# Accumulating weight transfers begun before and after the latent attention instead of inside it, and a planner that counts transfers as longer

## The chip, the cores and the metric

One core of a Trainium2 chip runs the whole program in one launch. The metric is device time in microseconds; the value compared is the median of the runs of a kernel. TensorE multiplies, VectorE, ScalarE and GpSimd work element by element, SyncE only issues transfers. The rows of the profile call them PE, DVE, ACT, POOL and SP.

## The reference

Two transformer blocks in float32 over 1024 tokens of width 1024. Block 1: a Fourier mixing and a latent attention (MLA, 8 heads) side by side, a cross attention over 256 memory tokens, and 16 experts that each choose 128 tokens. Block 2: one wide projection, a convolution of 31 taps per channel, dilated attention in three groups, gates. Cut to what the change touches:

```python
h = _rmsnorm(x, norm_g[layer]) * (1.0 + scale) + shift
proj = h @ w_in[layer]                       # block 2: 1024 x 10240
(glu_a, glu_b, z_conv, q, k, v, z_att, g_conv, g_att) = jnp.split(proj, split_idx, axis=-1)
```

## The kernel before

The kernel is written as a recording: each call on an engine becomes an operation with a price (line 236: time on its engine, and a latency until another engine can use the result). A list scheduler (line 284 on) then plays the program through with these prices and fixes, for each engine, one order of operations; on the chip each engine works its queue off in that order, and a wait at its head holds all that stands behind. So a changed price or a moved call changes orders far away too. A transfer that SyncE begins is priced with 2.0 us of latency, an accumulating one that GpSimd begins (`add_dma`) with 3.5 us. All operations recorded that way carry the line number 180 in the profile; the adding transfers carry 1433.

The order of stages is: block 1's input projection (`block1_in`) and Fourier part, MLA, output mixing (`mix_out`) and memory attention, routing and experts, and then block 2. There the projection is computed for sixteen pairs of tiles (`in2_pair`) by seven products of quarter matrices each, in place of eight, 112 products in all. Each product loads a quarter weight `wq`, ScalarE casts its high half into `wqs`, VectorE subtracts to get the low half (also `wqs`), and TensorE does twelve matmuls (four blocks of 128, three each: high by high, high by low, low by high) into one PSUM bank `wp`. VectorE then adds or subtracts `wp` to outputs named by their part (`glu_a`, `z_conv`, `z_att`, `g_att`). Between these operations VectorE also does the convolution's taps (`conv`), whose due time is set late by a constant, so they fill its gaps.

Four of the seven quarter weights of a pair are sums of quarters of the weight matrix. They are made in DRAM during block 1, since nothing needs them before block 2: for each pair a sum t13 = w2a + w2b and a sum t24 = w2a + w2d + w2c, half of which also gets a part of w_in. `weight_sums` is a generator that yields one step at a time: a copy of w2a (on SyncE's queue, 32 of them) or an accumulating transfer (on GpSimd's queue, 64 of them: 16 each of w2b, w2d, w2c and w_in). A sum's adds depend on each other, each begins when the one before has landed, and they wait at the head of GpSimd's queue. `sum_step(m)` takes the next m steps and stands at chosen places of the program. Before, the places are block 1's input projection (steps of 2 and 3), the Fourier loops (1) and each quarter of each MLA head (2, thirty-two times), and a last call takes what is left.

In MLA, GpSimd also scales the probabilities: for each head and each 128 queries TensorE computes scores `s`, the softmax gives `p` with its `sum`, GpSimd multiplies `p` by the reciprocal of the sum, TensorE transposes (`pt`) and multiplies by the values (`o`), which goes to `ya`. GpSimd also makes low halves of weights there (`wl`, `ql`, `kl`).

Of the kernel before, what the change touches and what calls it, by code (L numbers as in the profile page):

```python
# [188 lines left out]
class Program:  # L189
# [55 lines left out]
    def price(self, eng, fn, a, kw, wr, rd):  # L245

        out = wr[0] if wr else None
        if fn == "dma_start":
            v = next(x for x in list(a) + list(kw.values()) if isinstance(x, V))
            b = 4 * int(np.prod(v.shape))  # L250
            return max(0.45, b / 360e3), 2.0
        n = max([x.free for x in wr + rd if x is not None] or [1])
        if eng == "pe":
            m = rd[0]
# [339 lines left out]
class Kern(Program):  # L594
# [242 lines left out]
    def block1_in(self):  # L837
# [28 lines left out]
        for name, m0, n in (("q_lat", 4, 3), ("kv_lat", 7, 2)):  # L866
            tiles, acc = [], None
            for i in range(n):
# [9 lines left out]
                tiles.append((h, l))  # L878
                self.sum_step(2)
                if acc is not None:  # L880
# [41 lines left out]

        self.sum_step(2)
        self.uf = []
        for m in range(4):
            w = self.wtile(a["w_in"][m], 8)
            u = self.page("uf")
            self.gemm_t(w, xs, lambda t, ps: self.dve.tensor_tensor(u[:, t], ps, rxb[:, t], OP.mult), base="uf")
            self.out_dbg("uf", u, m)
            self.sum_step(3)  # L930
            self.uf.append(u)
# [107 lines left out]
    def mla(self):  # L1039
# [23 lines left out]
        for h in range(8):  # L1063
# [21 lines left out]
            for qq in range(4):  # L1085
                if 4 * h + qq in MEM_AT:
                    next(mem, None)
                self.sum_step(2)
                pth = [self.page("pth", F32R, (P, 4, 256)) for _ in range(2)]
# [25 lines left out]
        for _ in mem:  # L1115
            pass
        self.sum_step(1000)

# [14 lines left out]
    def mix_out(self, yf, x1d):  # L1133
# [5 lines left out]
        for m in range(8):  # L1139
# [4 lines left out]
            self.x1.append(x)  # L1144
            self.out_dbg("x1", x, m)

    def mem_stats(self):
# [46 lines left out]
    def mem_attention(self, x1d):  # L1194
# [8 lines left out]
        for m in range(8):  # L1203
# [4 lines left out]
            self.gemm_t(w, xs, lambda t, ps: self.act.copy(q[:, t], ps), base="mq")  # L1208
            qf.append(q)
            for _ in range(3):  # L1210
                n = len(self.ops)
                next(ada, None)
                for op in self.ops[n:]:
                    op.deps.add(n - 1)
# [11 lines left out]
        for hd in range(4):  # L1226
# [6 lines left out]
            for g in range(2):  # L1233
# [21 lines left out]
                for dm in range(2):  # L1255
# [6 lines left out]
                    self.split_to(oh[dm][0][:, t], oh[dm][1][:, t], o, lo="dve")  # L1262
            os[hd] = oh
            for part in PARTS:
                if part[-1] == hd:
# [164 lines left out]
    def add_dma(self, out, x):  # L1430

        def issue():
            self.nc.gpsimd.dma_start(out=out.ap(), in_=x.ap() if isinstance(x, V) else x, accum_op=OP.add,
                                     **({"max_dma_last_dim": 2048} if out.t.kind == "dram" else {}))
        op = self.record("pool", 1.0, 3.5, issue, [out] + [x] * isinstance(x, V), [out])
        op.dma = 4 * int(np.prod(out.shape)) / 180e3
        return op

    def sum_step(self, m):
        n = len(self.ops)  # L1440
        self.bias = 200
        for _ in range(m):
            next(self.sums, None)
        self.bias = 0
# [3 lines left out]
    def weight_sums(self):  # L1448


        a, n = self.a, len(PAIRS)
        self.t13 = [self.dram_tile((P, NT), "t13") for _ in PAIRS]
        self.t24 = [self.dram_tile((P, NT), "t24") for _ in PAIRS]
        R = slice(512, NT)
        for i in range(n + 3):
            if i < n:
                self.sp.dma_start(self.t13[i], a["w2a"][i], max_dma_last_dim=2048)
                yield
                self.sp.dma_start(self.t24[i], a["w2a"][i], max_dma_last_dim=2048)
                yield  # L1460
            if 0 <= i - 1 < n:
                self.add_dma(self.t13[i - 1], a["w2b"][i - 1])
                yield
                self.add_dma(self.t24[i - 1], a["w2d"][i - 1])
                yield
            if 0 <= i - 2 < n:
                self.add_dma(self.t24[i - 2], a["w2c"][i - 2])
                yield
            if 0 <= i - 3 < n:
                p, m = PAIRS[i - 3][0]  # L1470
                self.add_dma(self.t24[i - 3][:, R], a["w_in2"][IN2[p] + m][:, 4:].rearrange("p k c -> p (k c)"))
                yield

# [740 lines left out]
```

## Time and profile before

| | us |
|---|---|
| three runs | 2776.07, 2768.86, 2770.32 |
| median | 2770.32 |
| the profiled execution, its own time | 2776.95 |
| its span, first to last instruction | 2775.1 |
| TensorE busy in it | 2632.8 (95%) |
| VectorE, ScalarE, GpSimd busy | 2124.6, 1396.0, 497.8 |
| mean granted TensorE clock | 0.972 |

The rows further down come from this one execution. The windows view gives each engine's busy time and its count of instructions between two times of the span, with the granted clock. The waits view groups an engine's idle time by what it waited for. A timeline lists instructions with their start, length and, in brackets, the idle time before them and what ended it.

### The profile page before, as it was taken

The numbers are of one execution on the slowest core, as the hardware profiler recorded it, in microseconds if no ns is written. First come the engines' busy times: TensorE is split into PE (matmuls) and PEld (weight loads), VectorE is DVE, ScalarE is ACT, GpSimd is POOL, SyncE is SP. The second block draws the span as 40 slices with busy tenths as digits, with TensorE's granted clock in tenths as the row PEclk, the third lists the DMA queues.
The fourth block names the chain that finished last, engine by engine and source line by source line (L and its number), as shares of the span: only waits on it lengthen the run. The fifth ranks groups of instructions, "written<-read, shape, count | busy, mean of one in ns | idle before, by whom it ended". The sixth has DMA issues, their size and how long they took to land. (4 is left out here: it accounts for less than half of the span.)

```text
span 2775.1 us, 36565 instructions
## 1 busy us (share of the span) xinstructions
PE 2632.8 (95%) x13038; PEld 2202.8 (79%) x13038; DVE 2124.6 (77%) x3225; ACT 1396.0 (50%) x2280; POOL 497.8 (18%) x347
## 2 busy tenths in 40 slices
PE   8999989999994999999997999989999999998998
PEld 6888878888884888888876888768888887786877
DVE  7367876547666899988886998669999998669563
ACT  6156666432344777777776433334545455434211
POOL 2136558311004040000000000001111112001000
PEclk9999999999997999999998999999999999998999
DMA  7556565534537899999993333455556658678841
GB/s 243 145 123 121 131 157 140 193 109 155 200 107 278 316 345 366 351 374 374 391 346 118 114 114 120 139 158 127 135 133 137 148 128 244 161 215 300 320 171 53
DMA packets 178936, 555.18 MB, mean 200 GB/s; under 512 B 20179, under 2 KB 22419, under 8 KB 178753
## 3 DMA queue, kind: packets, MB, share of 16 engines
q1 hardware_dynamic: 150144, 481.53, 49.0%
q0 software_dynamic: 28608, 71.31, 14.0%
q8 instruction: 103, 1.69, 0.2%
q14 instruction: 81, 0.66, 0.1%
HBM read 439.02 MB, written 118.98 MB: 201 GB/s over the span
## 5 line engine op out<-in xcount | busy, mean ns | idle before, releaser
L180 DVE SCALAR_TENSOR_TENSOR conv<-glu_b,convw,conv 128x1023 f32<-128x1023 f32 (+14 forms) x210 | 268.0, 1277 | 2.6
L180 DVE TENSOR_TENSOR w_upl<-w_up,w_uph 128x1024 fp32r<-128x1024 f32 x128 | 149.2, 1220 | 23.0 <-ACT w_uph L180 22.4
L180 DVE TENSOR_TENSOR w_downl<-w_down,w_downh 128x1024 fp32r<-128x1024 f32 x128 | 149.0, 1219 | 13.5 <-ACT w_downh L180 12.9
L180 ACT CAST wqs<-wq 128x512 fp32r<-128x512 f32 x112 | 68.8, 621 | 167.6 <-PE wp L180 64.0
L180 DVE TENSOR_TENSOR w_gatel<-w_gate,w_gateh 128x1024 fp32r<-128x1024 f32 x123 | 144.0, 1218 | 7.5 <-ACT w_gateh L180 4.8
L180 PE MATMUL wp<-h2h,wqs 128*128 128x512 f32 x384 | 123.8, 396 | 9.6 <-ACT wqs L180 9.6
L180 ACT CAST w_gateh<-w_gate 128x1024 fp32r<-128x1024 f32 x128 | 125.6, 1053 | 6.4 <-issue 2.9
L180 ACT CAST w_downh<-w_down 128x1024 fp32r<-128x1024 f32 x128 | 126.0, 1055 | 1.4 <-PE ea L180 1.4
L180 ACT CAST w_uph<-w_up 128x1024 fp32r<-128x1024 f32 x128 | 125.8, 1055 | 1.4 <-PE ea L180 0.7
L180 ACT ACTIVATE ap<-ap,amx 128x128 f32<-128x128 f32 (+1 forms) x192 | 85.5, 449 | 68.9 <-DVE amx L180 62.0
L180 POOL MEMSET kl<- 64x1024 f32 x24 | 22.8, 951 | 475.5 <-PE wp L180 258.5
L180 POOL TENSOR_TENSOR wl<-w,wh 128x1024 fp32r<-128x1024 f32 (+3 forms) x31 | 61.7, 1990 | 244.5 <-ACT wh L180 227.5
L180 ACT CAST wh<-w 128x1024 fp32r<-128x1024 f32 (+3 forms) x71 | 62.4, 896 | 77.1 <-DMA w<-in_w_convout_dram 35.2
L180 DVE TENSOR_TENSOR ptl<-pt,pth 128x512 fp32r<-128x512 f32 x128 | 81.8, 683 | 19.5 <-ACT pth L180 12.9
L180 PEld LDWEIGHTS wp<-h2h,wqs 128*128 128x128 f32 x384 | 73.4, 191 | 25.9 <-ACT wqs L180 10.4
L180 ACT CAST w2h<-w 128x1024 fp32r<-128x1024 f32 x48 | 50.1, 1048 | 76.3 <-DMA w<-in_w_in_dram 60.3
L180 DVE TENSOR_TENSOR wqs<-wq,wqs 128x512 fp32r<-128x512 f32 x112 | 75.5, 685 | 16.5 <-ACT wqs L180 16.4
L180 ACT ACTIVATE p<-p,mx 128x1024 f32<-128x1024 f32 x64 | 73.8, 1155 | 26.1 <-DVE mx L180 17.5
L180 POOL TENSOR_SCALAR p<-p,sum 128x1024 f32<-128x1024 f32 x64 | 75.2, 1234 | 55.2 <-DVE sum L180 51.9
L180 PE MATMUL ea<-w_gatel,hth 128*128 128x512 f32 x256 | 80.1, 394 | 0.4 <-DVE w_gatel L180 0.4
L180 PE MATMUL ea<-w_gateh,hth 128*128 128x512 f32 x256 | 80.5, 395 | 0.0
L180 PE MATMUL eb<-w_uph,hth 128*128 128x512 f32 x256 | 80.5, 394 | 0.1
(626 smaller groups left out, 8623.0 us busy)
## 6 DMA issues: line engine op xcount, KB each, us to landing
w_gate<-in_w_gate_dram SPq DMA_DIRECT2D x128, 512.0 KB
w_up<-in_w_up_dram SPq DMA_DIRECT2D x128, 512.0 KB
w_down<-in_w_down_dram SPq DMA_DIRECT2D x128, 512.0 KB
w<-in_w_in_dram SPq DMA_DIRECT2D x57, 512.0 KB
w2l<-w POOLq DMA_DIRECT2D x36, 512.0 KB, 6.7
t<-in_w2a_dram SPq DMA_DIRECT2D x32, 512.0 KB
wq<-t SPq DMA_DIRECT2D x64, 256.0 KB
wada<-in_w_adaT_dram SPq DMA_DIRECT2D x24, 512.0 KB
```

The source lines that it names most:

```text
L180: getattr(k.engines[eng], fn)(*[r(x) for x in a], **{n: r(x) for n, x in kw.items()})
```

## The change

Five things are edited. The latency that the planner counts for a transfer goes from 2.0 to 2.8 us, that of an adding transfer from 3.5 to 5.5. The generator is split into one for copies and one for adds, and `sum_step` says from which it takes. Inside MLA only copies are taken, one for each quarter of a head. Adds are taken in block 1's later projection loop and the Fourier loops, and then after MLA: two for each of the eight tiles of `mix_out`, one for each of eight steps of the memory query projection, five after each of four memory heads. The last call, which took everything left, is gone. By the orders of the two kernels, 21 adds stand ahead of MLA before and 43 in it; of the changed kernel's 64, 20 stand ahead of it, none in it, and 44 behind it. Of the 32 copies, 14 then stand ahead of MLA and 18 in it.

```diff
         if fn == "dma_start":
...
-            return max(0.45, b / 360e3), 2.0
+            return max(0.45, b / 360e3), 2.8
...
                 self.gemm_t(w, xs, evac, base="u")
                 tiles.append((h, l))
-                self.sum_step(2)
+                self.sum_step(2, True)
...
-        self.sum_step(2)
+        self.sum_step(4, True)
         self.uf = []
         for m in range(4):
...
-            self.sum_step(3)
+            self.sum_step(2)
...
             for qq in range(4):
                 if 4 * h + qq in MEM_AT:
                     next(mem, None)
-                self.sum_step(2)
+                self.sum_step(1, True)
...
         for _ in mem:
             pass
-        self.sum_step(1000)
...
             self.out_dbg("x1", x, m)
+            self.sum_step(2)
...
             qf.append(q)
+            self.sum_step(1)
...
             os[hd] = oh
+            self.sum_step(5)
...
-        op = self.record("pool", 1.0, 3.5, issue, [out] + [x] * isinstance(x, V), [out])
+        op = self.record("pool", 1.0, 5.5, issue, [out] + [x] * isinstance(x, V), [out])
...
-    def sum_step(self, m):
+    def sum_step(self, m, copies=False):
         n = len(self.ops)
         self.bias = 200
         for _ in range(m):
-            next(self.sums, None)
+            next(self.sums[0 if copies else 1], None)
...
+        def copies():
+            for i in range(n):
+                for t in (self.t13, self.t24):
+                    self.sp.dma_start(t[i], a["w2a"][i], max_dma_last_dim=2048)
+                    yield
+
+        def adds():
+            for i in range(n + 2):
+                if i < n:
+                    self.add_dma(self.t13[i], a["w2b"][i])
+                    yield
+                    self.add_dma(self.t24[i], a["w2d"][i])
+                    yield
+                if 0 <= i - 1 < n:
+                    self.add_dma(self.t24[i - 1], a["w2c"][i - 1])
+                    yield
+                if 0 <= i - 2 < n:
+                    p, m = PAIRS[i - 2][0]
+                    self.add_dma(self.t24[i - 2][:, R], a["w_in2"][IN2[p] + m][:, 4:].rearrange("p k c -> p (k c)"))
+                    yield
+
+        return copies(), adds()
```

The adding transfers keep their own dependencies. The number of operations is the same; the orders of the engines differ. Three places follow.

GpSimd's queue inside MLA, in the kernel before. The first number of a tile's name tells tiles of one kind apart; the adds of one t24 have the same number:

```order
L180 TENSOR_SCALAR p_669_3095<-p_669_3095,sum_668_3120 128x1024
L1433 DMA t24_67_113<-in_w2d_dram 256x512
L1433 DMA t24_66_112<-in_w2c_dram 256x512
L1433 DMA t24_65_111<-in_w_in2_dram 128x512
L180 TENSOR_SCALAR p_676_3125<-p_676_3125,sum_675_3265 128x1024
L1433 DMA t13_52_98<-in_w2b_dram 256x512
L180 TENSOR_TENSOR ql_698_3296<-qf_694_3259,qh_697_3285 128x1024
L1433 DMA t24_68_114<-in_w2d_dram 256x512
L1433 DMA t24_67_113<-in_w2c_dram 256x512
L180 TENSOR_TENSOR wl_783_3350<-w_781_3279,wh_782_3310 128x384
L1433 DMA t24_67_113<-in_w_in2_dram 128x512
L180 TENSOR_SCALAR p_707_3359<-p_707_3359,sum_706_3387 128x1024
```

The same stretch in the changed kernel, with no adds:

```order
L180 TENSOR_SCALAR p_669_3029<-p_669_3029,sum_668_3094 128x1024
L180 TENSOR_TENSOR wl_783_3220<-w_781_3148,wh_782_3205 128x384
L180 TENSOR_SCALAR p_676_3068<-p_676_3068,sum_675_3238 128x1024
L180 TENSOR_TENSOR kl_690_3282<-kf_684_2858,kh_689_3266 128x1024
L180 TENSOR_TENSOR ql_698_3311<-qf_694_3263,qh_697_3294 128x1024
L180 TENSOR_TENSOR kl_780_3344<-kf_685_2867,kh_779_3276 128x1024
L180 TENSOR_TENSOR wl_820_3372<-w_818_3247,wh_819_3336 128x1024
L180 TENSOR_SCALAR p_707_3364<-p_707_3364,sum_706_3394 128x1024
L180 TENSOR_SCALAR p_714_3382<-p_714_3382,sum_713_3407 128x1024
```

The seven adds of the stretch are gone from it; low halves of weights (wl), keys (kl) and queries (ql) stand between the scalings of p instead.

VectorE's queue in block 2's quarter products, in the kernel before. The products follow each other on TensorE in the order of their numbers: wqs_3275 feeds wp_3276 (the 28th product), wqs_3278 feeds wp_3279 (29th), 3281 to 3282 (30th), 3284 to 3285 (31st), 3287 to 3288 (32nd):

```order
L180 TENSOR_TENSOR wqs_3284_14559<-wq_3283_14520,wqs_3284_14559 128x512
L180 SCALAR_TENSOR_TENSOR conv_3137_14217<-u_3126_13682,convw_139,conv_3137_14217 128x1007
L180 TENSOR_TENSOR z_conv_3249_14507<-wp_3268_14588,z_conv_3249_14507 128x512
L180 SCALAR_TENSOR_TENSOR z_conv_3250_14554<-th_3248_14599,z_conv_3250_14554 128x512 x2
L180 TENSOR_TENSOR wqs_3287_14578<-wq_3286_14534,wqs_3287_14578 128x512
L180 SCALAR_TENSOR_TENSOR z_conv_3249_14507<-th_3247_14620,z_conv_3249_14507 128x512
L180 TENSOR_TENSOR z_conv_3249_14507<-wp_3271_14607,z_conv_3249_14507 128x512
L180 SCALAR_TENSOR_TENSOR conv_3137_14217<-u_3126_13682,convw_139,conv_3137_14217 128x1006
L180 TENSOR_TENSOR wqs_3290_14628<-wq_3289_14542,wqs_3290_14628 128x512
L180 TENSOR_TENSOR wqs_3293_14639<-wq_3292_14566,wqs_3293_14639 128x512
L180 SCALAR_TENSOR_TENSOR conv_3137_14217<-u_3126_13682,convw_139,conv_3137_14217 128x1005
L180 SCALAR_TENSOR_TENSOR conv_3137_14217<-u_3126_13682,convw_139,conv_3137_14217 128x1004
```

And in the changed kernel, where wqs_3278 and two taps (128x1007 and 128x1006) stand right ahead of the first row, behind the read of wp_3271 (the 27th product):

```order
L180 SCALAR_TENSOR_TENSOR conv_3137_14209<-u_3126_13682,convw_139,conv_3137_14209 128x1005
L180 SCALAR_TENSOR_TENSOR conv_3137_14209<-u_3126_13682,convw_139,conv_3137_14209 128x1004
L180 SCALAR_TENSOR_TENSOR z_conv_3249_14514<-th_3247_14609,z_conv_3249_14514 128x512
L180 TENSOR_TENSOR wqs_3281_14629<-wq_3280_14449,wqs_3281_14629 128x512
L180 SCALAR_TENSOR_TENSOR conv_3137_14209<-u_3126_13682,convw_139,conv_3137_14209 128x1003
L180 SCALAR_TENSOR_TENSOR conv_3137_14209<-u_3126_13682,convw_139,conv_3137_14209 128x1002
L180 SCALAR_TENSOR_TENSOR conv_3137_14209<-u_3126_13682,convw_139,conv_3137_14209 128x1001
L180 TENSOR_TENSOR glu_a_3273_14688<-wp_3282_14663,glu_b_3272_14667 128x512
L180 SCALAR_TENSOR_TENSOR conv_3137_14209<-u_3126_13682,convw_139,conv_3137_14209 128x1000
L180 SCALAR_TENSOR_TENSOR conv_3137_14209<-u_3126_13682,convw_139,conv_3137_14209 128x999
L180 SCALAR_TENSOR_TENSOR conv_3137_14209<-u_3126_13682,convw_139,conv_3137_14209 128x998
L180 TENSOR_TENSOR wqs_3284_14679<-wq_3283_14487,wqs_3284_14679 128x512
```

The splits for the 31st and later products (wqs_3284 and on) stood ahead of the read of the 27th product's result (wp_3271) before; now that for the 30th stands behind four taps, and that for the 31st behind the read of the 30th product's result (wp_3282) and three more taps. Behind the last row shown come two taps and the split for the 32nd, then reads of products 31, 29 and 32, and behind the last of these the split for the 33rd.

VectorE's queue some forty products later, in the kernel before; wqs_3422 feeds the 70th product, wp_3418 is the result of the 69th:

```order
L180 TENSOR_TENSOR wqs_3422_15470<-wq_3421_15434,wqs_3422_15470 128x512
L180 TENSOR_TENSOR z_att_3396_15395<-wp_3415_15475,z_att_3396_15395 128x512
L180 SCALAR_TENSOR_TENSOR conv_3197_14881<-glu_b_3174_13998,convw_139,conv_3197_14881 128x1002
L180 SCALAR_TENSOR_TENSOR z_att_3397_15431<-th_3395_15491,z_att_3397_15431 128x512
L180 SCALAR_TENSOR_TENSOR z_att_3396_15395<-th_3394_15505,z_att_3396_15395 128x512
L180 TENSOR_TENSOR z_att_3396_15395<-wp_3418_15493,z_att_3396_15395 128x512
L180 SCALAR_TENSOR_TENSOR z_att_3397_15431<-th_3395_15491,z_att_3397_15431 128x512
L180 TENSOR_TENSOR wqs_3425_15512<-wq_3424_15443,wqs_3425_15512 128x512
```

In the changed kernel:

```order
L180 TENSOR_TENSOR z_att_3396_15392<-wp_3415_15473,z_att_3396_15392 128x512
L180 SCALAR_TENSOR_TENSOR conv_3197_14852<-glu_b_3174_13998,convw_139,conv_3197_14852 128x1002
L180 SCALAR_TENSOR_TENSOR z_att_3396_15392<-th_3394_15501,z_att_3396_15392 128x512
L180 TENSOR_TENSOR z_att_3396_15392<-wp_3418_15490,z_att_3396_15392 128x512
L180 SCALAR_TENSOR_TENSOR z_att_3397_15438<-th_3395_15507,z_att_3397_15438 128x512 x2
L180 SCALAR_TENSOR_TENSOR z_att_3396_15392<-th_3394_15501,z_att_3396_15392 128x512
L180 TENSOR_TENSOR wqs_3422_15518<-wq_3421_15423,wqs_3422_15518 128x512
```

The split wqs_3422 has moved from ahead of the read of wp_3418, and of the one before it, to a place behind it and behind three operations more; ScalarE's cast for it stands behind the tanh operations (th) that these need.

## Rows read from the trace of the kernel before

**Rows 1.** Windows by stage: stretch, length, busy time by engine (instructions), clock, DMA.

```profile
196.00:528.00 332.00, 314.21 (x1921) 274.72 (x1920) 248.06 (x551) 210.91 (x359) 206.02 (x152) 0.98 0.60 142
528.00:860.00 332.00, 330.84 (x1619) 277.06 (x1618) 192.57 (x285) 110.76 (x200) 30.15 (x12) 0.99 0.43 154
...
1500.00:1862.00 362.00, 349.68 (x1534) 286.30 (x1533) 295.66 (x399) 134.25 (x215) 7.56 (x8) 0.98 0.36 119
```

**Rows 2.** TensorE's waits, 196 to 530 us: waited for, us in total, times, longest.

```profile
PE pt L180 <- POOL p L180: 6.5, 4, 5.1
PE o L180 <- DVE ya L180: 2.8, 1, 2.8
```

**Rows 3.** Timeline of GpSimd, 341 to 356 us.

```profile
341.10 0.88 POOL L1433 DMA_DIRECT2D t<-in_w2d_dram  x1
341.70 1.18 POOL L1433 DMA_DIRECT2D t<-in_w2c_dram  x1
342.28 1.64 POOL L180 TENSOR_TENSOR wl<-w,wh 128x384 fp32r<-128x384 f32 x1
354.73 0.81 POOL L1433 DMA_DIRECT2D t<-in_w_in_dram  x1 [10.81 <-DMA t<-in_w2c_dram]
355.32 4.63 POOL L180 TENSOR_SCALAR p<-p,sum 128x1024 f32<-128x1024 f32 x4
```

**Rows 4.** Timeline of TensorE, 351 to 357 us.

```profile
351.08 0.61 PE L180 MATMUL s<-kl,qh 128*128 128x512 f32 x2
356.75 1.97 PE L180 MATMUL pt<-ident,p 128*128 128x128 f32 x8 [5.06 <-POOL p L180]
```

**Rows 5.** Windows, 355 to 365 us.

```profile
355.00:360.00 5.00, 3.25 (x13) 2.95 (x14) 1.62 (x3) 1.77 (x3) 4.95 (x5) 0.50 0.55 123
360.00:365.00 5.00, 5.00 (x38) 4.82 (x37) 4.24 (x13) 4.74 (x11) 2.22 (x2) 0.88 0.01 3
```

**Rows 6.** DMA issues: queue, count, KB each, median us from issue to landing.

```profile
t<-in_w2b_dram POOLq DMA_DIRECT2D x16, 512.0 KB, 7.4
t<-in_w2d_dram POOLq DMA_DIRECT2D x16, 512.0 KB, 8.7
t<-in_w2c_dram POOLq DMA_DIRECT2D x16, 512.0 KB, 9.4
```

**Rows 7.** TensorE's waits, 1500 to 1862 us.

```profile
PE wp L180 <- ACT wqs L180: 11.2, 5, 8.4
```

**Rows 8.** Windows, 1550 to 1600 us.

```profile
1550.00:1600.00 50.00, 50.00 (x223) 41.39 (x222) 46.52 (x64) 17.26 (x29) 1.33 (x2) 1.00 0.37 126
```

**Rows 9.** Timeline of VectorE, 1758 to 1763 us.

```profile
1758.23 0.69 DVE L180 TENSOR_TENSOR g_att<-wp,g_att 128x512 f32<-128x512 f32 x1 [1.96 <-PE wp L180]
1758.84 1.25 DVE L180 SCALAR_TENSOR_TENSOR conv<-glu_b,convw,conv 128x994 f32<-128x994 f32 x1
1760.01 0.68 DVE L180 TENSOR_TENSOR g_att<-wp,g_att 128x512 f32<-128x512 f32 x1
1760.61 0.68 DVE L180 SCALAR_TENSOR_TENSOR g_att<-wp,g_att 128x512 f32<-128x512 f32 x1
1761.20 2.05 DVE L180 TENSOR_TENSOR wqs<-wq,wqs 128x512 fp32r<-128x512 f32 x3
```

**Rows 10.** Timeline of TensorE, 1757 to 1766 us.

```profile
1757.81 0.39 PE L180 MATMUL wp<-s3h,wqs 128*128 128x512 f32 x1
...
1760.79 0.80 PE L180 MATMUL wp<-h2h,wqs 128*128 128x512 f32 x1 [1.15 <-ACT wqs L180]
...
1765.33 0.62 PE L180 MATMUL wp<-h2h,wqs 128*128 128x512 f32 x2
```

**Rows 11.** Windows, 1760 to 1765 us.

```profile
1760.00:1765.00 5.00, 4.21 (x11) 3.00 (x12) 3.18 (x6) 2.39 (x4) 0.00 (x0) 0.66 0.14 52
```

**Rows 12.** TensorE's waits, 1862 to 2440 us.

```profile
PE as L180 <- DMA ks<-ks: 6.4, 2, 4.8
...
PE q L180 <- DMA w2l<-w: 3.8, 2, 3.5
```

More of the change, by code (lines that the diff above doesn't have):

```diff
@@ L1454, in weight_sums @@
         R = slice(512, NT)
[L1455 to L1472, printed above, removed]
+        def copies():
[18 more added lines that the diff above has]
+        return copies(), adds()
     def tr8(self, x, base, n=8):
```

## The prediction

> **What bounds the kernel now.** First the windows by stage: in the latent attention (MLA, 196 to 528 us) TensorE is busy 314.21 of 332 us, in the mixing and memory-attention stretch (528 to 860) 330.84 of 332, in block 2's quarter products (1500 to 1862) 349.68 of 362 [rows 1]. So TensorE sets the time nearly everywhere, and an edit can gain only what TensorE now loses in waits and in the half-speed clock behind them. It can lose without such a limit, if a wait is put ahead of TensorE's weights. GpSimd is busy 206.02 of 332 us in MLA and 30.15 of the next 332 [rows 1]: the first stretch is where its queue is full.
>
> Next the waits of TensorE in MLA. The largest group is pt waiting for GpSimd's p, 6.5 us in four waits, 5.1 of it in one; then 2.8 for ya [rows 2]. The long one can be followed. GpSimd's queue has the add of w2d to a quarter sum at 341.10, of w2c to another at 341.70, a weight split wl, and then the add of w_in2 to the sum that w2c goes to. That add stands at the head of the queue until w2c has landed: 354.73, with 10.81 us of idle time ahead of it; p comes behind it at 355.32 [rows 3]. TensorE, whose last matmul starts at 351.08, resumes at 356.75, after 5.06 us idle on p [rows 4]. The granted clock is 0.50 for 355 to 360 and 0.88 for 360 to 365 [rows 5], the lower of two levels (1.2 against 2.4 GHz): about 6.2 us at half speed. TensorE works in that time from 356.75 to about 361.2, which is 4.45 us of work at half speed; half of it is lost, 2.2 us.
>
> **Part 1: no adds inside MLA.** Of 64 adds before, 43 stand inside MLA; after, none: 20 go ahead of it and 44 into the mixing and memory-attention stretch. The copies stay inside (18), but they go through SyncE's queue, on which nothing here waits. The wait above goes: 5.1 + 2.2 = 7.3 us. The other three waits for p are 1.4 us together and may go too. The limit is then 8.7 us. What is late next: p still waits for the softmax sums on VectorE, and the 2.8 us for ya [rows 2] has nothing to do with the adds. Since all the small waits of the stretch get a new order, I put back 2 to 3 us and take **−5 us** (bounds −9 and +2).
>
> **Part 2: 44 adds between MLA and the experts.** GpSimd is nearly free there (30.15 us), so issue costs nothing: 44 adds at the 0.6 us that one takes from start to start (341.10 to 341.70) are 26 us, of 332. But the adds of one sum wait for each other's landing, and the last ten form one run on GpSimd, ahead of wl_1579, the low half of a weight that TensorE needs. One landing took 7.4, 8.7 and 9.4 us in the median [rows 6], and 13.0 us in the place above (341.70 to 354.73). The last sum's adds need two landings one after another: 17 to 19 us, at worst 26, and some 5 us to issue the others and 2 us for the split itself. Between the last matmul of the fourth head's output and the first use of wl_1579 stand about 150 matmuls of 0.225 us (50.00 us for 223 [rows 8]), 34 us. So the cover holds up to about 13.5 us a landing. I take **+1 us**, for the new traffic beside weight loads; bounds 0 and +10.
>
> The row says 7 to 13 us for a landing of 512 KB. The Trainium skill ("DMA: Bandwidth & Descriptors", section "Anatomy of one DMA — SWDGE (gpsimd) path") has 2.0 us plus the bytes at 436 GB/s for a transfer that GpSimd begins, which gives an estimate of 3.2 us for 512 KB; by it the chain would be 6.4 us, and this rival would be gone. The trace disagrees by a factor of two to four, and the trace decides.
>
> **Part 3: the raised latencies move the whole plan.** The planner fixes each engine's queue. With loads counted 0.8 us longer it believes that block 2's quarter weights (wq) come later, and lays other VectorE work ahead of their split into wqs. On the chip a queue is in order: where an operation that reads the PSUM result of one product stands ahead of the split for the next product, TensorE has to wait. The queues show such places. One product is 12 matmuls, 2.7 us.
>
> A place of that kind exists in the trace of before, and gives the price. The operation that reads the last product starts on VectorE at 1758.23, a convolution tap at 1758.84, two more such reads at 1760.01 and 1760.61, and the splits at 1761.20 [rows 9]: 0.6 us each from start to start, a tap 1.17. TensorE's product ends with the matmul of 1757.81; the next product's first matmuls come early (1760.79), and the one after that stands 4.6 us behind what 2.7 us of work would need (1765.33 against 1758.04 + 2.70) [rows 10]. The clock in between was granted at 0.66 [rows 11]; of the 4.6 us some 3.0 are the wait less the early matmuls, 1.6 the slow clock.
>
> Place A, products 29 to 33. Time runs from the end of product 27; product 30 would be due at 5.4. Ahead of its split stand a read (0.2 + 0.6), the split for 29 (0.6), four taps (4.7) and another operation (0.6): 6.7, and with the split's own 0.7 and 0.15 to be seen, 7.5. So 2.1 us late, and product 30 ends at 10.2. Then VectorE reads product 30 (0.2 + 0.6), does three taps (3.5) and splits for product 31 (0.85): 15.4, a wait of 5.2. Product 32 waits 0.2 more; product 33 stands behind a read of 32 (0.2 + 0.6 + 0.85): 1.6. Sum 9.1, less about 1.3 for the two matmuls that each of three products can do with the high half alone, plus twice 1.6 for the clock: **11 us** (8 to 13).
>
> Place C, product 70: ahead of its split stand a read of product 69 (0.2 + 0.6), three more operations (1.8) and the split (0.85): 3.5 us, with the clock **5 us** (3 to 6). Four smaller places, each one read ahead of one split, 1.5 to 2 us each before the two early matmuls: **+4 us** (0 to 8). Of before's own 11.2 us of such waits in five [rows 7], the longest, 8.4 at the stage's end behind a reload, stays; of the others the place at 1758 goes, which with its clock is 4.6, and a lone wait of 0.7. Together 11 + 5 + 4 − 5.3 = **+14.7 us**, from +5 to +22.
>
> **Part 4: the rest.** In the dilated attention TensorE waits 6.4 us for ks and 3.8 for w2l, which an adding transfer makes [rows 12]. The order around them is nearly unchanged; I take **0**, bounds −6 and +5.
>
> **Sum:** −5 + 1 + 14.7 + 0 = +10.7 us. Against the profiled execution (2776.95 us, span 2775.1) that is 2787.6. That run is 6.6 us above the median of the three; the comparison goes by the median, so 2770.3 + 10.7 = **2781 us**. About 0.3%, 8.3 us, is what a measurement of this kernel can tell from no change: faster means under 2762.0, slower over 2778.6.
>
> **The rivals.**
> (a) The other side: the longer latencies do what they say. The waits for ks and w2l go (−10.2 at most, say −7), MLA gives its 8.7, and in the products the hi half and the early matmuls cover the smaller places, so that A and C cost 9 and the 5.3 is saved: +4. Sum −12: 2758. It decides where A and C together cost under 9 us. For it speaks that wl and p then stand in a free queue; against it, that a read of a product ahead of the next split is a wait in any case. Chance 0.15.
> (b) MLA's gain and the products' loss cancel: −8 + 8, 2770 (2763 to 2778). This needs A at its low end (8) and no small places. Chance 0.27.
> (c) The last run of adds makes wl_1579 late: landings over 13.5 us, as the one of 13.0 nearly was; at 15 us some 3 us, at 18 some 9 with the clock. 2781 + 9 = 2790. For it speaks the new crowding of 44 adds with weight loads; against it, the medians of 7 to 9 us. Chance 0.12.
> (d) The forecast, 2779 to 2787: chance 0.46, a hundredth of it at the lower bound's wrong side. The change does not do what it says only if adds remain in MLA, and none do.
>
> **The numbers.** Slower: (c), and (d) but for that hundredth: 0.57. Same: (b) and that hundredth: 0.28. Faster: (a): 0.15. For the range I leave out most of (a), below 2763, and what lies above (c)'s middle with A, C and the crowding all at their upper bounds, over 2797.
>
> **What would show it.** Right: in MLA no wait of GpSimd for t and pt waiting for p under 2 us; in the quarter products a row of TensorE waiting for wqs of about 5 us shortly after product 30, with two or three neighbours, and one of 3 us or so at product 70; the sum of wp waiting for wqs near 20 us. Wrong: those waits missing (then A's timeline fails, because TensorE was late for another reason), or the stretch from 528 to 860 longer by over 5 us (c), or the dilated attention shorter (a).

## The result and the profile after

The changed kernel takes 2787.72 us (median of five runs, 2785.6 to 2790.23) against 2770.8 of the kernel before in the same comparison: 1.0056 times as long, with a 95% interval of 1.0042 to 1.0071. The prediction was 2781 us, slower, with a range of 2763 to 2797. The profiled execution of the changed kernel took 2787.72 us itself, with a span of 2785.9, 10.8 us more than the span before. The one before was taken from a run 6 us above its median, so the stretches below add up to 10.8 and not to the 16.9 of the medians.

To see where it went, the program is cut at matmuls that both kernels have: the tile view gives, for one kind of matmul, the start of its first and its last. Of the kernel before, and then of the changed one (columns: shortest, median and longest duration in ns, then first and last start in us):

```profile
L180 PE MATMUL s<-kh,qh x128: 387/389/501, 206.9 to 506.8; 128*128 128x512 f32 x128
...
L180 PE MATMUL pt<-ident,p x512: 270/273/476, 217.4 to 518.9; 128*128 128x128 f32 x171
...
L180 PE MATMUL ea<-w_gateh,hth x256: 387/389/776, 904.5 to 1424.1; 128*128 128x512 f32 x128
...
L180 PE MATMUL wp<-h2h,wqs x384: 387/389/796, 1488.0 to 1859.9; 128*128 128x512 f32 x192
```

```profile
L180 PE MATMUL s<-kh,qh x128: 387/389/793, 208.7 to 498.2; 128*128 128x512 f32 x128
...
L180 PE MATMUL pt<-ident,p x512: 270/272/400, 219.3 to 516.6; 128*128 128x128 f32 x171
...
L180 PE MATMUL ea<-w_gateh,hth x256: 387/389/774, 906.5 to 1430.9; 128*128 128x512 f32 x128
...
L180 PE MATMUL wp<-h2h,wqs x384: 387/389/793, 1493.8 to 1882.7; 128*128 128x512 f32 x192
```

From these rows:

| stretch | before, us | after, us | difference | forecast |
|---|---|---|---|---|
| ahead of MLA's first s | 206.9 | 208.7 | +1.8 | |
| MLA, first s to last pt | 312.0 | 307.9 | −4.1 | −5 |
| mixing, memory attention, routing, to the first ea | 385.6 | 389.9 | +4.3 | +1 |
| experts, to the first wp | 583.5 | 587.3 | +3.8 | 0 |
| quarter products, first to last wp | 371.9 | 388.9 | +17.0 | +14.7 |
| dilated attention and the rest, to the end | 915.2 | 903.2 | −12.0 | 0 |

So the loss is in the quarter products, as forecast, and a gain of 12 us at the end was not forecast. First the quarter products. TensorE's waits in them, which answer to [rows 7], are 16.4 and 6.7 us where they were 11.2:

```profile
PE wp L180 <- ACT wqs L180: 16.4, 8, 6.9
PE wp L180 <- DVE wqs L180: 6.7, 4, 3.3
```

The three waits at place A, in TensorE's timeline. Products are counted from 0, as they were in the orders ahead, so product 30 is the 31st that TensorE starts; the first row is product 30 and the two others are product 31:

```profile
1627.11 0.74 PE L180 MATMUL wp<-s2h,wqs 128*128 128x512 f32 x2 [2.64 <-DVE wqs L180]
...
1631.83 0.50 PE L180 MATMUL wp<-s3h,wqs 128*128 128x512 f32 x1 [2.12 <-ACT wqs L180]
...
1635.84 1.22 PE L180 MATMUL wp<-s3h,wqs 128*128 128x512 f32 x2 [3.27 <-DVE wqs L180]
```

and VectorE's timeline there:

```profile
1620.68 5.16 DVE L180 SCALAR_TENSOR_TENSOR conv<-u,convw,conv 128x1007 f32<-128x1007 f32 x4
...
1626.36 0.69 DVE L180 TENSOR_TENSOR wqs<-wq,wqs 128x512 fp32r<-128x512 f32 x1
1626.97 3.85 DVE L180 SCALAR_TENSOR_TENSOR conv<-u,convw,conv 128x1003 f32<-128x1003 f32 x3
1630.74 0.68 DVE L180 TENSOR_TENSOR glu_a<-wp,glu_b 128x512 f32<-128x512 f32 x1
1631.34 3.84 DVE L180 SCALAR_TENSOR_TENSOR conv<-u,convw,conv 128x1000 f32<-128x1000 f32 x3
1635.10 0.68 DVE L180 TENSOR_TENSOR wqs<-wq,wqs 128x512 fp32r<-128x512 f32 x1
```

The four taps stand ahead of the split at 1626.36, for which product 30 waits 2.64 us; the read of product 30 and three taps stand ahead of the split at 1635.10, for which product 31 waits 3.27. Between these is a wait of 2.12 for a cast. It adds nothing to the delay, since the split for the same product comes only at 1635.10, and VectorE has no idle time ahead of it from 1620.68 on; but it shows where the order comes from. ScalarE's cast for product 31:

```profile
1631.16 0.62 ACT L180 CAST wqs<-wq 128x512 fp32r<-128x512 f32 x1 [4.04 <-DMA z_conv<-z_conv]
```

The last thing that it waits for is not the raw weight that it reads but a store of z_conv to DRAM, which holds the page of SBUF into which the cast writes. The large tiles of this kernel share 50 pages, and the planner says which page a tile gets. The clock falls behind the waits (granted clock is the third number from the end):

```profile
1630.00:1635.00 5.00, 0.73 (x2) 0.30 (x2) 4.93 (x5) 0.62 (x1) 0.00 (x0) 0.78 0.08 32
1635.00:1640.00 5.00, 4.17 (x11) 3.31 (x12) 3.80 (x5) 1.24 (x2) 0.00 (x0) 0.54 0.00 0
```

Product 30 began at 1623.85, so three products later, at 2.7 us each, product 33 was due at 1631.95; it began at 1642.72: 10.8 us.

Place C, product 70, has the wait too:

```profile
1748.63 0.66 PE L180 MATMUL wp<-h2h,wqs 128*128 128x512 f32 x1 [3.36 <-ACT wqs L180]
```

The products ahead of it end at 1745.1 and the one behind it starts at 1753.07, 5.3 us more than 2.7.

In MLA the wait for p has gone from 6.5 to 1.6 us [rows 2], but others have come, one of 3.6 for qf among them:

```profile
PE s L180 <- DVE qf L180: 3.6, 1, 3.6
PE o L180 <- DVE ptl L180: 2.5, 5, 1.4
PE pt L180 <- DVE mx L180: 1.7, 2, 1.0
PE pt L180 <- POOL p L180: 1.6, 2, 1.1
```

The adds behind MLA land later than they did [rows 6] (median us from issue to landing at the end of each line):

```profile
t<-in_w2b_dram POOLq DMA_DIRECT2D x16, 512.0 KB, 10.8
t<-in_w2d_dram POOLq DMA_DIRECT2D x16, 512.0 KB, 10.3
t<-in_w2c_dram POOLq DMA_DIRECT2D x16, 512.0 KB, 13.2
```

The last run of them on GpSimd is the chain of which rival (c) spoke:

```profile
753.44 2.21 POOL L1435 DMA_DIRECT2D t<-in_w2d_dram  x1
...
768.15 0.88 POOL L1435 DMA_DIRECT2D t<-in_w2c_dram  x1 [7.07 <-DMA t<-in_w2d_dram]
...
778.52 0.81 POOL L1435 DMA_DIRECT2D t<-in_w_in_dram  x1 [5.81 <-DMA t<-in_w2c_dram]
```

One landing took 14.7 us, the other 10.4, and the run ended at 778.5. The weight split behind it began only at 816.23, after 36.9 us in which it waited for TensorE and not for an add; TensorE has no wait for such a split in this stretch:

```profile
816.23 2.41 POOL L180 TENSOR_TENSOR wl<-w,wh 128x1024 fp32r<-128x1024 f32 x1 [36.90 <-PE lg L180]
```

### The profile page after: what moved, and what is told of

Its sections match the earlier page's. It is cut to its first block, busy times and chain, and to the rows that moved or that the text cites. A ratio compares the mean times of both kernels' runs of the same rounds, so it can differ in the third digit from the quotient of the medians.

```text
span 2785.9 us, 36560 instructions
## 1 busy us (share of the span) xinstructions
PE 2635.3 (95%) x13038; PEld 2199.8 (79%) x13038; DVE 2108.6 (76%) x3225; ACT 1400.0 (50%) x2280; POOL 481.7 (17%) x347
## 5 line engine op out<-in xcount | busy, mean ns | idle before, releaser
L180 DVE SCALAR_TENSOR_TENSOR conv<-glu_b,convw,conv 128x1023 f32<-128x1023 f32 (+15 forms) x210 | 264.9, 1266 | 2.2
L180 PE MATMUL wp<-h2h,wqs 128*128 128x512 f32 x384 | 125.0, 399 | 11.1 <-ACT wqs L180 10.7
L180 ACT CAST wh<-w 128x1024 fp32r<-128x1024 f32 (+3 forms) x71 | 63.0, 895 | 84.7 <-DMA w<-in_w_convout_dram 35.3
L1427 POOL DMA_INDIRECT x<-ey,idx x16 | 25.4, 1588 | 320.2 <-ACT ey L180 185.0
```

The source lines that it names most:

```text
L180: getattr(k.engines[eng], fn)(*[r(x) for x in a], **{n: r(x) for n, x in kw.items()})
L1427: self.nc.gpsimd.indirect_dma_start(out=rows.ap(), out_offset=bass.IndirectOffsetOnAxis(ap=idx.ap(), axis=0), in_=x.ap(), in_offset=None, ...
```

## The experiments

Ratios are to the kernel before in the same comparison, with 95% intervals; the stretches, in us, are cut as in the table above, and come from one profiled execution of each.

| run | ratio | MLA | to ea | experts | wp | wp to end |
|---|---|---|---|---|---|---|
| before | 1 | 312.0 | 385.6 | 583.5 | 371.9 | 915.2 |
| changed | 1.0056 (1.0042 to 1.0071) | 307.9 | 389.9 | 587.3 | 388.9 | 903.2 |
| e1, adds moved only | 0.9972 (0.9958 to 0.9985) | 299.5 | 386.9 | 581.9 | 371.7 | 915.6 |
| e2, latencies only | 1.0083 (1.0065 to 1.0100) | 312.6 | 392.3 | 589.0 | 390.8 | 904.0 |
| e4, moved, adds at 5.5 | 0.9982 (0.9965 to 0.9998) | 300.3 | 388.2 | 583.4 | 369.4 | 917.2 |
| e5, changed, wq at 2.0 | 1.0004 (0.9992 to 1.0016) | 308.6 | 386.0 | 587.7 | 377.3 | 903.6 |
| e7, changed, loads 7 ahead | 1.0027 (1.0016 to 1.0038) | 307.9 | 386.8 | 587.2 | 379.2 | 900.0 |
| e8, before, one add later | 0.9985 (0.9972 to 0.9999) | 308.0 | 385.8 | 582.7 | 372.2 | 911.9 |
| e9, moved, wq at 2.8 | 0.9985 (0.9970 to 1.0000) | 300.4 | 387.2 | 581.7 | 376.5 | 913.2 |
| e10, moved, 2.8 late | 0.9918 (0.9904 to 0.9931) | 300.5 | 388.0 | 581.1 | 369.1 | 897.6 |
| e11, e10 with adds at 5.5 late | 0.9928 (0.9911 to 0.9945) | 300.4 | 384.9 | 582.1 | 369.0 | 904.9 |
| e12, before, no adds in MLA | 0.9952 (0.9940 to 0.9965) | 302.8 | 386.7 | 582.1 | 368.9 | 909.8 |

How far one execution of a stretch can be trusted, kernels with the same order there show: e8 and e12 have that of the kernel before behind MLA; e5 and e7 have that of the changed kernel, and e9, e10 and e11 that of e1, up to the quarter products, e10 and e11 through them. Among these, MLA differs by up to 1.0 us, the stretch to the first ea by 3.9, the experts by 1.4, the quarter products by 3.3 and the stretch to the end by 5.4. Against the median of its kernel the profiled execution lies 6.7 us above in e2 and 8.6 below in e7; for the kernel before it lies 2 to 3 above the medians of these comparisons (2774.01 to 2775.21), and in the others within 4.3.

**e1 and e2: each half alone.** e1 is the changed kernel with the old latencies, and e2 the kernel before with the new ones. The edit of e1, against the changed kernel (e2 is the reverse, on the kernel before):

```diff
-            return max(0.45, b / 360e3), 2.8
+            return max(0.45, b / 360e3), 2.0
...
-        op = self.record("pool", 1.0, 5.5, issue, [out] + [x] * isinstance(x, V), [out])
+        op = self.record("pool", 1.0, 3.5, issue, [out] + [x] * isinstance(x, V), [out])
```

> The adds moved as in the changed kernel, both latencies as before (2.0 and 3.5). Stretches: pairs (first to last matmul of wp) 371.9 us before, 388.9 changed; MLA (first s to last pt) 312.0 and 307.9; between last pt and first ea 385.6 and 389.9; from the last wp to the end 915.2 and 903.2. Theory: the loss in the pairs comes from the latency counted for transfers, not from the moved adds. Then pairs 370 to 374, MLA 306 to 310, between 388 to 391, median 2764 to 2772. Rival, the adds' new place disturbs what follows: pairs 380 or more, median over 2777.

> Both latencies raised (2.8 and 5.5), the adds where they were, inside MLA. Theory: pairs 386 to 391 (the same three waits of 2 to 3.5 us around the 30th product), MLA 310 to 315 with a wait for p of some 5 us in it, between 385 to 387, median 2784 to 2792. Rival, only both edits together make the loss: pairs under 376, median under 2776.

The halves pull in opposite directions. The moved adds alone are faster than the kernel before (2765.93 against 2774.01 us), the latencies alone slower by 22 us (2796.31). Multiplied, 0.9972 and 1.0083 give 1.0055, which is the change's 1.0056 within its interval. The quarter products keep 371.7 with the old latencies and take 390.8 with the new ones, at place A with waits like those of the changed kernel (TensorE's timeline of e2):

```profile
1640.38 1.22 PE L180 MATMUL wp<-s2h,wqs 128*128 128x512 f32 x2 [2.64 <-DVE wqs L180]
...
1645.11 0.50 PE L180 MATMUL wp<-s3h,wqs 128*128 128x512 f32 x1 [0.69 <-ACT wqs L180]
...
1649.63 1.22 PE L180 MATMUL wp<-s3h,wqs 128*128 128x512 f32 x2 [3.79 <-DVE wqs L180]
```

Two things were not expected. MLA gains 12.5 us with the adds moved, more than the 2 to 6 that were expected, and only 4 of them are left when the latencies go up too. And the stretch behind the quarter products is 11 us shorter in e2, with nothing moved.

**e5, e9 and e7: why the quarter products lose.** e5 is the changed kernel with one price put back, that of the loads of raw quarter weights; its edit is shown. e9 is e1 with that one price raised:

```diff
-            return max(0.45, b / 360e3), 2.8
+            return max(0.45, b / 360e3), 2.0 if out is not None and out.t.name.startswith('wq_') else 2.8
```

> The changed kernel, but the planner counts 2.0 us for the loads of block 2's quarter weights (wq) alone; every other transfer stays at 2.8, the adds at 5.5. Theory, the latency of these loads alone makes the loss, since raw weights then hold pages of SBUF longer and the split weights wait for pages: pairs 371 to 376, no wait for wqs over 1 us around the 30th product, all else as in the changed kernel, median 2768 to 2776. Rival, the later return of pages behind stores (z_conv), which keep 2.8 here, makes it: pairs 384 or more, median 2783 to 2790.

> The adds moved, all transfers counted as before (2.0 and 3.5) but the loads of the quarter weights wq at 2.8. Theory, the latency of these loads is enough for the loss: pairs 385 or more, ratio over 1.002. Rival, it needs both, longer loads and pages that stores give back later: pairs 372 to 380, no wait over 2 us around the 30th product, ratio 0.996 to 1.000.

With the price of these loads put back, the waits at places A and C are gone and the stretch is 377.3 (a little over what was expected; a wait like that of [rows 9] is back around product 81, and 2.6 us near product 94 stay). So the loads' price is needed for the loss. It is not enough: raised alone, the stretch takes 376.5 and place A has no wait (there is a new one of 3.79 near product 73). It needs the longer price of other transfers beside it, the stores that give pages back among them; which, these runs don't separate.

e7 leaves all prices as changed, and ties a load to the end of the product seven ahead of it, so that raw weights cannot fill pages early:

```diff
+            n0 = len(self.ops)
             raw = self.load(src[wn], "wq", (P, 4, P))
+            self.ends4 = getattr(self, "ends4", [])
+            if len(self.ends4) >= 7:
+                self.ops[n0].deps.add(self.ends4[-7])
...
+            self.ends4.append(len(self.ops) - 1)
             self.turn4 += TICK4
```

> The changed kernel with all its latencies; only, the load of a quarter weight is not issued before the product seven ahead of it is done (in the changed kernel the planner lets it go some eleven products ahead). Theory, the loads that run ahead take the pages that the splits need: the three waits around the 30th product (8.0 us with their neighbours' slow clock about 11) go, a place like that of rows 9 comes back around the 81st product (some 4.5 us), pairs 378 to 384, median 2776 to 2783. Rival, the order of VectorE has nothing to do with pages taken early: pairs 386 or more, median 2785 or more.

379.2 us, no wait for wqs at place A, 0.71 and 0.80 left at place C, and a wait around product 81 (TensorE's timeline of e7):

```profile
1764.15 0.50 PE L180 MATMUL wp<-s4h,wqs 128*128 128x512 f32 x1 [0.71 <-ACT wqs L180]
...
1766.04 0.50 PE L180 MATMUL wp<-h2h,wqs 128*128 128x512 f32 x1 [1.15 <-ACT wqs L180]
```

It shows that place A can be removed by holding the loads back alone. The profiled execution of e7 is its fastest, but by the medians too it is faster than the changed kernel (1.0027 against 1.0056).

The planner's own times, which the scheduler gives when the code of each kernel is played through without the chip, show the reason. In the plan of the changed kernel the raw weight of product 31 is ready for its cast at 1548.8 us of planned time, and a page for the result only at 1574.8, behind the store of z_conv that the trace shows; 11 raw weights hold pages when the product starts. In the plan of before these are 1540.9, 1542.5 and 5 raw weights; in that of e7 the page is free ahead of the weight, and 2 raw weights hold pages. At place C it is the same: the weight of product 70 is ready at 1678.2, and a page, until then that of a tanh, at 1686.3. So the splits are put late since their pages are late, and taps, which need no new page, are put ahead of them. The plan even holds the loss itself:

| quarter products, us | before | changed | e1 | e2 | e5 | e7 | e9 | e10 |
|---|---|---|---|---|---|---|---|---|
| planned | 363.0 | 388.3 | 363.0 | 388.3 | 371.5 | 377.2 | 373.8 | 363.0 |
| measured | 371.9 | 388.9 | 371.7 | 390.8 | 377.3 | 379.2 | 376.5 | 369.1 |

**e8 and e12: what the adds cost MLA.** e8 is the kernel before with one change in GpSimd's queue, the add of [rows 3] behind the next four scalings of p. e12 is the kernel before in its own order with the 43 adds inside MLA left out and nothing in their place; block 2's quarter sums lack them, so its time is not that of the whole computation. The edits of e8 and e12, cut:

```diff
+def later(order):
...
+    at = {o.i: n for n, o in enumerate(order)}
+    op = order[at[2805]]
...
+    order.remove(op)
+    order.insert(next(n for n, o in enumerate(order) if o.i == 2594) + 1, op)
```

> The kernel before, with one adding transfer (the one of rows 3 that waits 10.81 us at the head of GpSimd's queue) moved behind the next four scalings of p. Theory of the prediction: that wait of 5.06 us and the slow clock behind it are 7.3 us; MLA 304 to 307 instead of 312.0, ratio 0.997 to 0.998. Rival, the next wait takes its place: MLA 309 or more, ratio 0.999 or more.

```diff
-                op.fn()
+                if not op.left_out:
+                    op.fn()
...
+        op.left_out = self.phase == 1 and out.t.kind == "dram"
```

> The kernel before, in its order, with the 43 adding transfers inside MLA left out and nothing in their place (so block 2's quarter sums lack them). It prices the adds inside MLA by themselves; the one long wait was 4.0 us. Theory, the adds cost MLA more than that wait, by GpSimd's queue and traffic: MLA 299 to 304 instead of 312.0, as with the adds moved (299.5). Rival, most of those 12.5 us come from the new order that the planner finds without them: MLA 305 to 309, as with the one add moved (308.0).

e8 takes the wait away, and MLA gains 4.0 us, between the two theories and not the 7.3 of the prediction. GpSimd scales p while the add of w2c is still in flight, and the add behind it then waits 0.38 us in place of 10.81 (GpSimd's timeline of e8):

```profile
348.28 1.13 POOL L180 TENSOR_SCALAR p<-p,sum 128x1024 f32<-128x1024 f32 x1 [5.96 <-DVE sum L180]
...
351.29 2.22 POOL L180 TENSOR_SCALAR p<-p,sum 128x1024 f32<-128x1024 f32 x2 [0.39 <-PE pt L180]
353.89 0.83 POOL L1433 DMA_DIRECT2D t<-in_w_in_dram  x1 [0.38 <-DMA t<-in_w2c_dram]
```

But TensorE, which no longer waits 5.06 us on p, waits 1.70 for ptl at almost the same place, and the granted clock there is still 0.66 for 355 to 360, against 0.50 [rows 5] (TensorE's timeline of e8, then the windows view):

```profile
355.33 0.76 PE L180 MATMUL pt<-ident,p 128*128 128x128 f32 x4 [1.70 <-DVE ptl L180]
```

```profile
355.00:360.00 5.00, 4.52 (x24) 4.08 (x25) 5.00 (x15) 4.75 (x9) 2.33 (x3) 0.66 0.44 61
```

Without any of the 43 adds MLA takes 302.8 us, 9.2 less, and TensorE waits 0.3 us for p. That is most of e1's 12.5; the rest of these may be the new order, or the difference between two executions. Whether the adds cost it by holding GpSimd's queue or by their traffic, e12 does not separate.

**e4, e10 and e11: where the 12 us at the end come from.** e4 is e1 with the adding transfers counted at 5.5. It asks if the gain comes from their price, since adding transfers also make the low halves w2l in the dilated attention.

> The adds moved, the adding transfers counted at 5.5 us, all others at 2.0. Theory: the gain behind the pairs (last wp to the last q matmul 528.0 before, 532.6 with the moved adds alone, 518 to 521 wherever both latencies were raised) comes from the adding transfers of the low halves w2l, which are then begun earlier; pairs 371 to 374, MLA 298 to 302, that stretch 518 to 524, median 5 to 12 us under that of the moved adds alone (ratio to before 0.992 to 0.996). Rival, that gain comes from the 2.8 us of the loads: that stretch 528 or more, ratio 0.997 like the moved adds alone.

It is not: 917.2 us, as with the old prices, and no gain in the total over e1 (0.9982 against 0.9972). That leaves the 2.8 us. e10 keeps 2.0 up to the end of the quarter products and uses 2.8 behind them; e11 also counts 5.5 for the adding transfers there. The edit of e10, against e1:

```diff
+    dma_lat = 2.0
...
-            return max(0.45, b / 360e3), 2.0
+            return max(0.45, b / 360e3), self.dma_lat
...
                 self.gate_pair(i, gd)
+        self.dma_lat = 2.8
         n = len(self.ops)
```

> The adds moved; transfers counted at 2.0 up to the end of the quarter products and at 2.8 from the dilated attention on, adds at 3.5 throughout. Theory: the gain behind the pairs (last wp to the end 915.2 us before, 915.6 with the moved adds alone, 900.0 to 904.0 in the four kernels with 2.8) belongs to the 2.8 us in that stage, the losses (MLA +8, experts +5, pairs +17) to the 2.8 ahead of it. Then MLA 299 to 301, pairs 370 to 373, last wp to end 900 to 906, ratio to before 0.992 to 0.995. Rival, that stretch was only another order that depends on what lies ahead: 911 to 918, ratio 0.997 as with the moved adds alone.

> As the run with 2.8 from the dilated attention on, and the adding transfers there at 5.5. Theory: the adding transfers matter only with the loads at 2.8; last wp to end 898 to 904, ratio 0.991 to 0.995. Rival, the adds' 5.5 do nothing or harm, as they did with loads at 2.0 (917.2): 905 to 917, ratio 0.995 to 0.998.

e10 takes 2750.49 us, 24.7 less than the kernel before in its comparison (2775.21) and less than anything else here. Its stretch to the end is 897.6 us, as short as with 2.8 throughout (900.0 to 904.0) or shorter, and MLA (300.5), the experts (581.1) and the quarter products (369.1) are as with 2.0. e11 shows nothing of its own: 904.9 to the end, on the border between its two theories, and 0.9928, where the intervals overlap. Over all runs the six with 2.8 in the last stretch take 897.6 to 904.9 there, the six with 2.0 take 909.8 to 917.2; the two groups do not meet. In the dilated attention of e10 the wait for w2l [rows 12], 3.8 us before, is no longer among TensorE's waits:

```profile
PE as L180 <- DMA ks<-ks: 4.9, 2, 3.0
PE as L180 <- issue: 4.3, 3, 2.0
PE g_conv L180 <- ACT w2h L180: 3.7, 1, 3.7
...
```

Over the whole stretch to the end TensorE is idle for 35.3 us in e10 and 45.5 before. From the windows view, e10, then before, then the changed kernel, where it is idle for 37.9 (length, then TensorE's busy time):

```profile
1847.50:2745.10 897.60, 862.27 (x4336) 721.79 (x4334) 715.47 (x1242) 372.63 (x808) 98.82 (x86) 0.98 0.64 179
```

```profile
1859.90:2775.10 915.20, 869.75 (x4336) 726.49 (x4335) 721.57 (x1242) 371.26 (x809) 101.46 (x85) 0.98 0.62 176
```

```profile
1882.70:2785.90 903.20, 865.35 (x4336) 726.36 (x4334) 713.73 (x1242) 373.77 (x808) 102.53 (x86) 0.98 0.63 178
```

The other 7.5 of the 17.6 us are TensorE's busy time for the same 4336 recorded matmuls. Less time at the slow clock fits that: the mean clock of the two rows, 0.98 in both, is too coarse to show it, but over windows of 5 us the length times what the granted clock lacks to 1 adds up to 22.6 us before and 16.0 in e10, 6.6 less.

## Why the prediction was right, and where it was not

**Sign and size.** Slower was right, and 2787.7 lies in the range, 6.7 us above the value. Term by term it was less right than that looks: an error of 12 us in one direction was met by smaller ones in the other, which come to the same sum. That the spans differ by 10.8, next to the 10.7 of the forecast, is luck; the medians differ by 16.9. Of the signs that it named, those of being right came: no wait of GpSimd for an add in MLA, 1.6 us of waits for p, the rows at products 30 and 70, and 23.1 us of waits for wqs in all. One sign of being wrong, that of (a), came too: from the last wp to the last q of the dilated attention it is 521.1 us, where it was 528.0 (q of before, then of the changed kernel):

```profile
L180 PE MATMUL q<-h2h,w2h x144: 387/389/796, 1860.2 to 2387.9; 128*128 128x512 f32 x144
```

```profile
L180 PE MATMUL q<-h2h,w2h x144: 387/389/628, 1882.9 to 2403.8; 128*128 128x512 f32 x144
```

**Part 3, the quarter products,** carried the forecast and held: +17.0 against +14.7. Place A cost 10.8 us by TensorE's starts (forecast 11), place C 5.3 (forecast 5). Counting start-to-start times of operations that stand in a row on VectorE, from the end of the product that the first one reads, was enough for both. The 0.9 us that is left of the 17.0 holds the place at 1758, which went, against smaller waits, the longest 2.60 near product 94. The reason given was wrong in part. The planner does not put other work ahead because it believes the weights to come late; in its plan the raw weights are there early and hold pages, and the casts and splits wait for pages, 26.0 us at product 31. That is why one of place A's waits, 2.12 us, was for a cast and not for the split (cast held 4.04 us by the store), and why e7 removes the place without touching a latency.

**Part 1, MLA,** was −4.1 against −5, by two errors. The single wait was priced at 7.3 us and is worth 4.0 (e8): the step "the wait above goes" counted all of the wait and of the slow clock, and the next wait, 1.70 for ptl, and a clock of 0.66 stayed. The limit of 8.7 us was no limit either: MLA is 9.2 shorter without the adds (e12) and 12.5 with them moved at the old prices (e1). On the other side the 2 to 3 us "put back" for the new order were 8, and they come with the prices: MLA takes 299.5 to 300.5 in the five runs with moved adds and 2.0 ahead of it, and 307.9 to 308.6 in the three with 2.8. With the adds left inside, the prices cost MLA nothing (e2, 312.6); with the adds moved the plan has 5.5 us of the 8 (301.4 us for MLA in the changed kernel, 295.9 in e1), and the reason stays open.

**Part 2, the adds behind MLA,** was +1. The stretch is +4.3 in the execution of the changed kernel, but +0.4 and +1.2 in e5 and e7, which have its order there, and +1.3 in e1 with the adds alone (386.9); that is within what executions differ by, and does not speak against +1. The landings went from 7.4 to 9.4 up to 10.3 to 13.2 us, one to 14.7, past the 13.5 from which rival (c) was to decide. It still did not happen: behind the run the split waited 37 us for TensorE. The cover was counted from the last matmul of the fourth head's output (mo), where the adds were assumed to begin, and that step was too careful: the run of ten began at 751.22, 50 us ahead of it (GpSimd's timeline, then the tile view):

```profile
751.22 0.87 POOL L1435 DMA_DIRECT2D t<-in_w2d_dram  x1
```

```profile
L180 PE MATMUL mo<-mpth,mvl x32: 387/390/398, 713.4 to 801.3; 128*128 128x512 f32 x32
```

The estimate of 3.2 us for such a landing, from the Trainium skill's "DMA: Bandwidth & Descriptors" (section "Anatomy of one DMA — SWDGE (gpsimd) path"), is further off here than it was before: the rows show 10.3 to 14.7.

**Part 4 failed.** The order around the dilated attention was called nearly unchanged and given 0, bounds −6 to +5; the stretch to the end is 12.0 us shorter. By e10 against e1 the 2.8 us in that stage makes it, so this half of rival (a) came true, but not by the waits that (a) named. Those for ks and w2l were to go; together they are 10.8 us in the changed kernel where they were 10.2, w2l less and ks more (waits of the changed kernel, to compare with [rows 12]):

```profile
PE as L180 <- DMA ks<-ks: 9.9, 4, 3.8
...
PE q L180 <- DMA w2l<-w: 0.9, 1, 0.9
```

The 7.6 us less of idle time is spread over many small waits, and how the price brings it about is not shown; the planner's own times don't have this gain (833.2 us for the stretch in e10, 833.7 before). The experts, also given 0, lose about 4 to 5 us with 2.8 (587.2 to 589.0 in four runs, 581.1 to 583.5 in the eight others). Two of these us are waits for the low half of a gate weight, 0.4 before and 2.4 in the changed kernel (before, then changed):

```profile
PE ea L180 <- DVE w_gatel L180: 0.4, 1, 0.4
```

```profile
PE ea L180 <- DVE w_gatel L180: 2.4, 5, 0.5
```

## What to carry to other kernels

A latency in a planner's prices is a setting of one stage. The same 0.8 us more gained some 12 us in the last stage and lost 17 where buffers were short; setting it by stage (e10) took the gain without the loss, and testing the two halves of an edit apart led there. And where a planner shares out buffers, look at which buffer an operation writes and who holds it, before explaining the order by the data it reads. The planner's own times say that without a run: here they held a loss in the quarter products, of 25.3 us, where 17.0 were measured.

## What was not expected of the hardware

An adding transfer of 512 KB from DRAM to DRAM took 7.4 to 9.4 us from issue to landing in the median of a kind in the kernel before, with 43 of all 64 adds in MLA, and 10.3 to 13.2 in the changed kernel, with 44 behind it. The DMA engines are busier there (0.74 of the stretch from MLA to the first ea, against 0.60 in MLA before [rows 1]); that this is the reason is not shown. The 43 adds cost a stage that TensorE fills to 95% about 9 us (e12), of which the one visible long wait was 4.
